# Values of three attention layers in plain fp32 on two 64-column tiles, with new call orders

## Chip, cores and metric

The kernel runs on one core of a Trainium2 chip. The metric is the device time of one launch in microseconds (us), as the median of several runs. The core has a matrix engine (TensorE, "PE" in the profile, its weight loads "PEld"), VectorE ("DVE"), ScalarE ("ACT"), GpSimd ("POOL") and SyncE ("SP").

## What is computed

One inference step of a backbone with four layers over 640 tokens (512 latent tokens, 128 context tokens) of 1024 features. Layers 0 and 3 have mixer A (sliding window, grouped queries, a sink logit per head), layer 1 mixer B (latent attention), layer 2 mixer C (normalised queries and keys, full attention over the latent tokens and the context). Each is followed by a squared-ReLU MLP; shift, scale and gate come from a conditioning vector (adaLN). All is fp32. The core of a mixer, cut to what matters here:

```
def attend(q, k, v, scale, sink=None, mask=None):
    s = jnp.einsum('bqhgd,bkhd->bhgqk', q, k) * scale
    if mask is not None:
        s = jnp.where(mask, s, NEG_INF)
    ...                       # softmax over keys, with the sink column
    return jnp.einsum('bhgqk,bkhd->bqhgd', p.astype(v.dtype), v)

for i in range(DEPTH):
    ...
    hp = modulate(rmsnorm(xp, norm_g[i, 0]), sh_p, sc_p)
    hs = modulate(rmsnorm(xs, norm_g[i, 0]), sh_s, sc_s)
    if kind == 0:
        op, k_ctx, v_ctx = mixer_a_context(hp, a_w_qkv[j], a_sink[j], a_w_o[j])
        os_ = mixer_a_latent(hs, cache_a_k[:, j], cache_a_v[:, j], a_w_qkv[j], a_sink[j], a_w_o[j], rows, cols)
    ...
    xs = xs + gt_s * os_
    xs = xs + gt2_s * sq_relu_mlp(modulate(rmsnorm(xs, norm_g[i, 1]), sh2_s, sc2_s), w_mlp_in[i], w_mlp_out[i])
```

There are 16 query heads of 64 features and 4 key/value heads; in mixer A a block of 128 queries sees at most three blocks of 128 latent keys and one of 128 context keys.

## The kernel before

**Split products.** Almost every matrix product is made of two-part numbers: an operand x is held as hi (a copy rounded to the type fp32r, one pass through TensorE) and lo = x - hi (also fp32r), and a product is three matmuls, hi·hi, hi·lo and lo·hi, into one accumulator. The hi part is made by a copy on ScalarE, the lo part by a subtraction on VectorE. Weights are loaded into `wraw`, split into pairs of tiles `wa`, and feed matmuls of 320 tokens (two halves of the 640).

**Attention of kinds A and C.** The sixteen heads are handled as eight pairs, class `Pair`. The steps of a pair: `qk` (scores), `mx`, `ex`, `rc`, `sc` (row maximum, exponential, reciprocal, scaling; GpSimd has a part of the scaling), then for each head e and group g of key blocks `tr` (transpose of the probabilities on TensorE into a PSUM bank of the pool `tb`), `hi` and `lo` (the split of the transposed tile from PSUM into two arena tiles), and `pv` (the product with the values, accumulated in the bank `V` over both heads of the pair). Kind A has four groups with together five key blocks of 512, 256, 256, 384 and 384 query columns per head; kind C has five groups of 512. The steps that begin with `z` do the same for the 128 context queries (`zt` transposes, `zh` and `zl` split, `zv` multiplies, `za` and `zb` put the result away, once for each head). `oh` and `ol` split the pair's output for the output projection. `fw`, `fh` and `fl` load and split weights of that projection meanwhile.

**Where the values lie.** In kind A the values of a key block are split into `VH` and `VL` with columns of zeros between the heads, so that a 128-column weight tile holds one head's 64 columns and 64 zeros, and both heads add into one bank of 128 partitions; a product is three matmuls. In kind C, `VS` holds the hi and lo columns of one head side by side (128 columns), so two matmuls do, and `pa` (ScalarE) and `pb` (VectorE) add the two halves afterwards; `ol` is on GpSimd there.

**What sets the order.** Calls to the engines are recorded by `Calls.keep` and made in another order by `replay`: for each phase ("0 qkv", "0 attn", "0 oproj" and so on) a table `ORDER` of written-out numbers gives the order, on all engines at once. In a phase of attention the calls are recorded in the order that `PLAN` gives: a list of steps, each with a lag in rounds behind the round's pair (`tr00.2` is worked for the pair two rounds back), and the table acts on that. Each engine then works through its own list in this order and waits where data isn't there. Since the calls are made in one place, all instructions in the trace have the line of `make`, L276, and are told apart by their tiles: `p` probabilities, `cst` the identity for transposes, `ar` arena tiles of 128 x 640, `ps` and `psl` PSUM banks, `x` the residual stream, `adaw` and `junk` adaLN weights and their reductions on VectorE.

Of the kernel before, what the change touches and what calls it, by code (L numbers as in the profile page):

```python
# [12 lines left out]
F32 = mybir.dt.float32  # L13
# [16 lines left out]
WCAP = 6  # L30
KIND = "ABCA"
# [10 lines left out]
ORDER = {  # L42
    "0 attn": """
# [19 lines left out]
    """,  # L63
    "0 oproj": """
# [9 lines left out]
    """,  # L74
    "0 qkv2": """
# [4 lines left out]
    """,  # L80
    "0 qkv": """
# [5 lines left out]
    """,  # L87
    "0 start": """
# [4 lines left out]
    """,  # L93
    "1 dq": """
# [108 lines left out]
    """,  # L203
}
ORDER = {n: [int(i) for i in o.split()] for n, o in ORDER.items()}

# [1554 lines left out]
```

## Time and profile before

| | us |
|---|---|
| median of 3 runs | 3064.46 (3064.37 to 3067.91) |
| profiled execution, own time | 3069.06 |
| its span | 3067.3 |
| TensorE busy | 2962.0 |
| VectorE busy | 2122.7 |
| ScalarE busy | 1339.0 |
| GpSimd busy | 548.0 |

The mean granted clock of TensorE over the profiled execution is 0.991 of full. The stages on the time axis: start and projections of layer 0 until about 154, its attention until 260, output projection and MLP until about 780; layer 1 until about 1590; layer 2's projections until 1699, its attention until about 1830, its MLP until about 2290; layer 3's projections until 2438, its attention until 2542, then its MLP and the end. A row of the timeline is a run of like instructions of one engine: start, duration from the first start to the last end, engine, line, operation, output<-inputs, rows*columns of the tile of TensorE, shape of the moving data, count, and in brackets the idle time ahead of it and what ended it. Records of matmuls overlap, since matmuls are pipelined: the distance between starts tells their price, not their durations. A plain fp32 matmul leaves two records, one of fp32r leaves one.

### The profile page before, as it was taken

How to read it: one execution, taken by the hardware profiler on the slowest of the kernel's cores; microseconds unless marked ns; L12 is line 12 of the kernel's file. 1: busy time of each engine (PE TensorE's matmuls, PEld its weight loads, DVE VectorE, ACT ScalarE, POOL GpSimd, SP SyncE). 2: the span in 40 equal slices, each digit the busy share in tenths (PEclk: the TensorE clock that was granted, in tenths of full speed). 3: DMA queues.
4: the chain of work that ended last, by engine and by line, in shares of the span. 5: the costliest groups of instructions: out<-in, count | busy, mean ns of one | idle time of the engine just before them, and what ended most of it. 6: DMA issues, size and time to landing. Idle time of an engine off the chain costs nothing. (4 is left out here: it accounts for less than half of the span.)

```text
span 3067.3 us, 52256 instructions
## 1 busy us (share of the span) xinstructions
PE 2962.0 (97%) x20250; PEld 2884.7 (94%) x20250; DVE 2122.7 (69%) x4605; ACT 1339.0 (44%) x2836; POOL 548.0 (18%) x713
## 2 busy tenths in 40 slices
PE   6999999999999999999998999999999999999998
PEld 4888999999999989999997889999999899999998
DVE  5696767666788887767469988776747896533434
ACT  3384522323487753322347883332233593322331
POOL 1162000000044341000003660000000370000000
PEclk9999999999999999999999999999999999999999
DMA  8303344442121134444211013444431102222221
GB/s 300 130 1 124 103 145 152 149 149 96 40 60 47 37 125 163 147 152 148 84 55 45 10 43 118 146 150 152 144 93 49 46 1 83 90 72 74 76 76 49
DMA packets 88602, 300.72 MB, mean 98 GB/s; under 512 B 10977, under 2 KB 15281, under 8 KB 87969
## 3 DMA queue, kind: packets, MB, share of 16 engines
q1 hardware_dynamic: 64112, 210.22, 20.6%
q0 software_dynamic: 24240, 87.16, 8.7%
q8 instruction: 159, 2.61, 0.3%
q14 instruction: 91, 0.74, 0.1%
HBM read 288.53 MB, written 3.56 MB: 95 GB/s over the span
## 5 line engine op out<-in xcount | busy, mean ns | idle before, releaser
L276 PE MATMUL ps<-ar,wa 128*128 128x320 f32 x6736 | 1139.2, 311 | 16.4 <-DVE wa L276 8.7
L276 PE MATMUL psl<-ar,wa 128*128 128x320 f32 x6408 | 1084.3, 310 | 1.9 <-DVE ar L276 1.6
L276 PEld LDWEIGHTS ps<-ar,wa 128*128 128x128 f32 x6736 | 1030.0, 189 | 20.9 <-DVE wa L276 9.5
L276 PEld LDWEIGHTS psl<-ar,wa 128*128 128x128 f32 x6408 | 979.4, 188 | 3.4 <-DVE ar L276 2.3
L276 ACT ACTIVATE wa<-wraw 128x1024 fp32r<-128x1024 f32 (+3 forms) x350 | 360.0, 1030 | 965.2 <-PE psl L276 440.2
L276 DVE TENSOR_TENSOR wa<-wraw,wa 128x1024 fp32r<-128x1024 f32 (+3 forms) x346 | 416.7, 1204 | 291.8 <-ACT wa L276 290.8
L276 DVE CUSTOM_DVE_ANT_0 junk<-adaw,cb 128x1024 bf16<-128x1024 f32 x304 | 373.4, 1228 | 9.4 <-DMA adaw<-ada 8.9
L276 PE MATMUL psl<-ex,wa 128*128 128x320 f32 x1320 | 322.9, 314 | 5.1 <-DVE wa L276 2.0
L276 PE MATMUL ps<-ex,wa 128*128 128x320 f32 x1304 | 318.1, 313 | 5.5 <-DVE wa L276 3.3
L276 POOL TENSOR_TENSOR p<-p,st 128x640 f32<-128x640 f32 (+2 forms) x256 | 277.0, 1104 | 180.0 <-DVE st L276 144.7
L276 POOL DMA_DIRECT2D adaw<-ada x152 | 80.5, 530 | 1051.4 <-DVE mod L276 983.9
L276 PE MATMUL psl<-wa,ar 128*128 128x320 f32 (+3 forms) x1024 | 236.2, 335 | 17.0 <-DVE st L276 7.5
L276 PEld LDWEIGHTS psl<-ex,wa 128*128 128x128 f32 x1320 | 229.1, 189 | 9.4 <-DVE wa L276 2.3
L276 DVE TENSOR_TENSOR ar<-ps,ar 128x512 fp32r<-128x512 f32 (+3 forms) x416 | 223.2, 560 | 19.8 <-ACT ar L276 16.3
L276 PEld LDWEIGHTS ps<-ex,wa 128*128 128x128 f32 x1304 | 225.5, 189 | 9.8 <-DVE wa L276 4.2
L276 ACT ACTIVATE ar<-ps 128x512 fp32r<-128x512 f32 (+5 forms) x452 | 208.5, 489 | 56.1 <-PE ps L276 50.7
L276 DVE SCALAR_TENSOR_TENSOR x<-ps,mod,x 128x320 f32<-128x320 f32 (+2 forms) x264 | 107.2, 436 | 180.8 <-PE ps L276 180.6
L276 DVE SCALAR_TENSOR_TENSOR x<-psl,mod,x 128x320 f32<-128x320 f32 (+2 forms) x240 | 98.7, 436 | 192.3 <-PE psl L276 192.2
L276 ACT ACTIVATE p<-p,st 128x640 f32<-128x640 f32 (+2 forms) x256 | 190.6, 748 | 18.7 <-DVE st L276 8.6
L276 PEld LDWEIGHTS psl<-wa,ar 128*128 128x128 f32 x1024 | 166.0, 193 | 30.7 <-DVE st L276 14.9
L276 PE MATMUL ps<-cst,p 128*128 128x128 f32 x1088 | 155.2, 274 | 5.6 <-DVE wa L276 2.6
L276 DVE TENSOR_TENSOR usq<-relu 128x320 f32<-128x320 f32 x256 | 124.5, 487 | 44.5 <-ACT relu L276 42.6
(205 smaller groups left out, 2817.6 us busy)
## 6 DMA issues: line engine op xcount, KB each, us to landing
adaw<-ada POOLq DMA_DIRECT2D x152, 512.0 KB, 4.3
wraw<-win SPq DMA_DIRECT2D x128, 512.0 KB, 3.3
wraw<-wout SPq DMA_DIRECT2D x128, 512.0 KB, 3.3
wraw<-qkv SPq DMA_DIRECT2D x36, 512.0 KB, 3.6
wa<-adan SPq DMA_DIRECT2D x24, 512.0 KB, 5.1
wraw<-wo SPq DMA_DIRECT2D x24, 512.0 KB, 3.7
adaw<-ada SPq DMA_DIRECT2D x16, 512.0 KB, 8.4
ar<-wa SPq DMA_DIRECT2D x64, 80.0 KB, 2.1
```

The source lines that it names most:

```text
L276: return m(*a, **k)
```

## The change

In the attentions of layers 0, 2 and 3 neither the values nor the transposed probabilities are split. The values lie in one fp32 tile `V` of 128 x 6 x 256, written by one copy on ScalarE per token block and by the transfer of the cached values directly. A transposed group is copied once, by step `cp`, from PSUM into an fp32 tile of a new pool `pt` (eight arena tiles turned to fp32 and `PT` = 5 or 6 new ones): odd groups on VectorE, even groups on ScalarE. `pv` is one step for the whole pair: plain fp32 matmuls whose weight tile is the 64 columns of one head, with the two heads of the pair alternating and writing to partitions 0 to 63 and 64 to 127 of the same bank. `zc`, `zv`, `za` and `zb` are made alike. `oh` and `ol` read the bank, `ol` on VectorE in both kinds. The zero columns, `VS` and the adding of halves are gone from kinds A and C; class `PairB` (layer 1) keeps the split steps.

```
+PT = {"A": 5, "C": 6}
...
+    def cp(self, e, g):
+        t = self.T[e, g]
+        ps = t[0]
+        t[0] = self.k.pt.popleft()
+        if g % 2:
+            self.nc.vector.tensor_copy(out=t[0][:, :t[1]], in_=ps[:, :t[1]])
+        else:
+            self.nc.scalar.activation(t[0][:, :t[1]], ps[:, :t[1]], AF.Copy)
+        self.k.tb.append(ps)
+
+    def pv(self):
+        k, nc = self.k, self.nc
+        self.V = k.vb.popleft()
+        last = {"A": 3, "C": 4}[k.kind]
+        for g in range(last + 1):
+            G = self.groups(g)
+            o = 0
+            for i, (kb, b0, b1) in enumerate(G):
+                n = (b1 - b0) * P
+                for e in (0, 1):
+                    nc.tensor.matmul(self.V[64 * e:64 * e + 64, b0 * P:b1 * P], self.v(kb, e), self.T[e, g][0][:, o:o + n], start=g + i == 0, stop=g == last and i == len(G) - 1)
+                o += n
+            k.pt += [self.T.pop((e, g))[0] for e in (0, 1)]
+
+    def v(self, kb, e):
+        c = (self.pr // 4 * 2 + e) * 64
+        return self.k.V[:, kb, c:c + 64]
...
+    def zc(self):
+        self.zt_ = self.k.pt.popleft()
+        self.nc.scalar.activation(self.zt_[:, :256], self.ZT[:, :256], AF.Copy)
+        self.k.tb.append(self.ZT)
+
+    def zv(self):
+        k = self.k
+        o = self.ZO = k.tb.popleft()
+        for e in (0, 1):
+            self.nc.tensor.matmul(o[64 * e:64 * e + 64, :P], self.v(5, e), self.zt_[:, e * P:e * P + P], start=True, stop=True)
+        k.pt.append(self.zt_)
...
                 def values():
-                    cv, sv = csv or (cks(), self.rps()[:, :256])
-                    nc.gpsimd.dma_start(cv, a["cv"][l])
+                    nc.gpsimd.dma_start(self.V[:, 2, :], a["cv"][l])
...
-                        if tb < 4:
-                            self.v_put(KB_OF_TB[tb], ps[:, :256])
-                        else:
-                            nc.scalar.activation(sv, ps[:, :256], AF.Copy)
-                            nc.gpsimd.dma_start(a["sv"][l], sv)
-                            self.v_put(5, sv)
+                        nc.scalar.activation(self.V[:, KB_OF_TB[tb], :], ps[:, :256], AF.Copy)
+                        if tb == 4:
+                            nc.gpsimd.dma_start(a["sv"][l], self.V[:, 5, :])
```

`PLAN` for kinds A and C is rewritten with the new steps; the largest lag falls from four rounds to three. The table of every phase of `ORDER` is new, except "2 oproj" and "3 oproj", which are the same, and layer 1's attention keeps its plan.

What moves, on TensorE in layer 0's attention, in the middle of a round, before (`VH` and `VL` the split values, `ar` the split probabilities, `cst,p` transposes, `psl` scores):

```order
L276 MATMUL ps_72<-cst,p_4_1466 128x128 x2
L276 MATMUL ps_74<-ar_95,VH_487 128x384
L276 MATMUL ps_74<-ar_94,VH_487 128x384
L276 MATMUL ps_74<-ar_94,VL_488 128x384
L276 MATMUL psl_1_79<-wa_111,ar_99 128x512
L276 MATMUL psl_1_79<-wa_113,ar_99 128x512
L276 MATMUL ps_74<-ar_83,VH_487 128x384
L276 MATMUL ps_74<-ar_82,VH_487 128x384
L276 MATMUL ps_74<-ar_82,VL_488 128x384
```

and after:

```order
L261 MATMUL ps_73<-cst,z_0_1474 128x128 x2
L261 MATMUL ps_74<-ar_1461,V_487 64x512
L261 MATMUL ps_74<-ar_1465,V_487 64x512
L261 MATMUL ps_74<-ar_1462,V_487 64x256
L261 MATMUL ps_74<-ar_1466,V_487 64x256
L261 MATMUL ps_74<-ar_1462,V_487 64x256
L261 MATMUL ps_74<-ar_1466,V_487 64x256
L261 MATMUL ps_74<-ar_1463,V_487 64x384
L261 MATMUL ps_74<-ar_1467,V_487 64x384
L261 MATMUL ps_74<-ar_1464,V_487 64x384
L261 MATMUL ps_74<-ar_1468,V_487 64x384
L261 MATMUL ps_72<-t_0_1469,V_487 64x128 x2
```

The products with the values, spread before between transposes and scores in threes, now stand in one block of ten and two more for the context.

On VectorE at the end of layer 0's attention and the start of its output projection, before (`junk` with `ISA` a reduction for adaLN, `wa<-wraw` the lo part of a projection weight):

```order
L276 TENSOR_TENSOR wa_117<-wraw_1_62,wa_116 128x1024
L276 TENSOR_TENSOR ar_83<-ps_72,ar_82 128x384
L276 TENSOR_TENSOR ar_85<-ps_73,ar_84 128x256
L276 TENSOR_TENSOR ar_109<-ps_71,ar_108 64x128
L276 TENSOR_TENSOR ar_87<-ps_74,ar_86 128x512
L276 TENSOR_TENSOR ar_87<-ps_72,ar_86 64x128 x2
L276 ISA junk,mod_0_169<-adaw_0_2674,cb 128x1024
```

and after:

```order
L261 TENSOR_TENSOR wa_117<-wraw_1_62,wa_116 128x1024
L261 COPY t_2_1471<-ps_73 128x384
L261 TENSOR_TENSOR wa_993<-wraw_0_61,wa_992 128x1024
L261 TENSOR_TENSOR ar_105<-ps_74,ar_104 128x512
L261 TENSOR_TENSOR ar_105<-ps_72,ar_104 128x128
L261 TENSOR_TENSOR wa_111<-wraw_0_61,wa_110 128x1024
L261 ISA junk,mod_0_169<-adaw_0_2428,cb 128x1024
```

Behind the last row eight reductions follow in both; before, two weight splits (the one shown and one three rows ahead of it) stand close ahead of them, after, three, the last of them next to the reductions.

On ScalarE in layer 3's projections, where the value weights are split, before (`wa<-wraw` the hi part of a weight, `ar<-rpq` and `rpq` the rotary chain of queries and keys):

```order
L276 ACTIVATE wa_1005<-wraw_0_61 128x1024
L276 ACTIVATE ar_85<-rpq_1_21711 64x320
L276 ACTIVATE ar_84<-rpq_1_21711 64x320
L276 ACTIVATE ar_96<-rpq_0_21710 64x320
L276 ACTIVATE ar_97<-rpq_0_21710 64x320
L276 ACTIVATE rpq_1_21711<-psl_3_17223 128x128
L276 ACTIVATE ar_97<-rpq_1_21711 64x320
L276 ACTIVATE ar_96<-rpq_1_21711 64x320
L276 ACTIVATE wa_110<-wraw_1_62 128x1024
```

and after:

```order
L261 ACTIVATE ar_106<-rpq_0_21242 64x320
L261 ACTIVATE ar_107<-rpq_0_21242 64x320
L261 ACTIVATE wa_994<-wraw_0_61 128x1024
L261 ACTIVATE rpq_1_21243<-psl_1_16750 128x128
L261 ACTIVATE wa_110<-wraw_1_62 128x1024
L261 ACTIVATE ar_107<-rpq_1_21243 64x320
L261 ACTIVATE ar_106<-rpq_1_21243 64x320
```

The two copies of the value weights stood with seven operations of the rotary chain between them; now there is one.

## Rows read from the trace of the kernel before

**Rows 1.** The page, busy us, share of the span and instructions of each engine.

```profile
PE 2962.0 (97%) x20250; PEld 2884.7 (94%) x20250; DVE 2122.7 (69%) x4605; ACT 1339.0 (44%) x2836; POOL 548.0 (18%) x713
```

**Rows 2.** Stretches: window, length, busy PE PEld DVE ACT POOL, granted clock, DMA.

```profile
170.00:250.00 80.00, 79.12 (x527) 71.36 (x526) 74.34 (x235) 72.88 (x208) 58.12 (x90) 1.00 0.01 1
1712.00:1820.00 108.00, 107.03 (x703) 94.69 (x702) 105.49 (x274) 105.84 (x250) 81.47 (x71) 1.00 0.02 6
```

**Rows 3.** Timeline of TensorE in layer 0's attention: start, us, instructions.

```profile
217.37 0.64 PE L276 MATMUL ps<-ar,VH 128*128 128x512 f32 x2
...
218.08 0.49 PE L276 MATMUL ps<-cst,p 128*128 128x128 f32 x3
...
225.87 0.40 PE L276 MATMUL ps<-ar,VH 128*128 128x256 f32 x2
...
226.22 0.60 PE L276 MATMUL ps<-cst,p 128*128 128x128 f32 x4
226.57 0.49 PE L276 MATMUL ps<-ar,VH 128*128 128x256 f32 x2
...
227.02 0.51 PE L276 MATMUL ps<-ar,VH 128*128 128x384 f32 x2
...
227.54 0.51 PE L276 MATMUL ps<-ar,VH 128*128 128x384 f32 x2
```

**Rows 4.** Timeline of TensorE and its weight loads at adaLN matmuls on column tiles.

```profile
29.85 0.64 PE L276 MATMUL ps<-adaw,cs 128*32 128x256 f32 x8 [3.10 <-DMA adaw<-ada]
...
54.34 1.34 PE L276 MATMUL psl<-ar,wa 128*128 128x320 f32 x8
55.60 1.07 PE L276 MATMUL ps<-wa,cs 128*32 128x256 f32 x16
56.60 0.41 PE L276 MATMUL ps<-ex,wa 128*128 128x320 f32 x1
56.85 0.31 PE L276 MATMUL ps<-ar,wa 128*128 128x320 f32 x1
...
55.60 0.59 PEld L276 LDWEIGHTS ps<-wa,cs 128*32 128x32 f32 x16 [0.19 <-issue]
56.60 0.19 PEld L276 LDWEIGHTS ps<-ex,wa 128*128 128x128 f32 x1 [0.41 <-ACT ar L276]
```

**Rows 5.** Groups by shape: out<-in, count | busy us, mean ns | idle before.

```profile
L276 DVE TENSOR_TENSOR ar<-ps,ar 128x512 fp32r<-128x512 f32 x224 | 148.7, 683 | 11.5 <-ACT ar L276 9.9
L276 ACT ACTIVATE ar<-ps 128x512 fp32r<-128x512 f32 x224 | 128.2, 594 | 30.9 <-PE ps L276 27.3 <-ACT ar L276 0.6 <-ACT p L276 0.5
```

**Rows 6.** Timeline of TensorE and VectorE at the start of layer 0's output projection.

```profile
281.09 13.11 PE L276 MATMUL ps<-ar,wa 128*128 128x320 f32 x70 [6.66 <-DVE wa L276]
...
278.67 1.22 DVE L276 CUSTOM_DVE_ANT_0 junk<-adaw,cb 128x1024 bf16<-128x1024 f32 x1
...
279.82 1.22 DVE L276 TENSOR_TENSOR wa<-wraw,wa 128x1024 fp32r<-128x1024 f32 x1
```

**Rows 7.** Timeline of TensorE at layer 3's values.

```profile
2422.20 1.44 PE L276 MATMUL psl<-wa,ar 128*128 128x256 f32 x3 [3.27 <-ACT wa L276]
2425.01 2.72 PE L276 MATMUL psl<-wa,ar 128*128 128x256 f32 x11 [1.38 <-DVE wa L276]
```

**Rows 8.** Timeline of TensorE at the first scores of layer 2's attention.

```profile
1699.30 1.92 PE L276 MATMUL psl<-wa,ar 128*128 128x320 f32 x8 [3.52 <-DVE VS L276]
```

**Rows 9.** Timeline of TensorE and VectorE at layer 0's last query columns.

```profile
144.21 0.90 PE L276 MATMUL ps<-ex,wa 128*128 128x320 f32 x2 [3.34 <-DVE wa L276]
...
142.94 1.22 DVE L276 TENSOR_TENSOR wa<-wraw,wa 128x1024 fp32r<-128x1024 f32 x1
```

**Rows 10.** Stretches with half clock: window, length, busy PE PEld DVE ACT POOL, clock, DMA.

```profile
144.00:150.00 6.00, 5.79 (x22) 5.80 (x23) 4.82 (x12) 2.15 (x5) 1.64 (x2) 0.50 0.29 87
1699.00:1707.00 8.00, 6.77 (x25) 5.85 (x26) 4.65 (x13) 3.73 (x9) 1.18 (x1) 0.57 0.00 1
2422.00:2430.00 8.00, 6.42 (x26) 5.70 (x27) 5.48 (x12) 3.10 (x8) 1.17 (x2) 0.50 0.29 84
```

More of the change, by code (lines that the diff above doesn't have):

```diff
@@ L42 @@
 ORDER = {
-    "0 attn": """
[19 rows of a table removed]
+    "1 dq": """
[6 rows of a table added]
+    """,
+    "3 attn": """
[15 rows of a table added]
+    """,
+    "2 attn": """
[15 rows of a table added]
+    """,
+    "0 attn": """
[15 rows of a table added]
+    """,
+    "1 oproj": """
[9 rows of a table added]
+    """,
+    "3 qkv": """
[9 rows of a table added]
+    """,
+    "2 qkv": """
[13 rows of a table added]
+    """,
+    "0 qkv": """
[5 rows of a table added]
     """,
     "0 oproj": """
[9 rows of a table removed]
[9 rows of a table added]
     """,
     "0 qkv2": """
[4 rows of a table removed]
-    """,
-    "0 qkv": """
[5 rows of a table removed]
[4 rows of a table added]
     """,
     "0 start": """
[4 rows of a table removed]
-    """,
-    "1 dq": """
[6 rows of a table removed]
-    """,
-    "1 oproj": """
[9 rows of a table removed]
-    """,
-    "2 attn": """
[21 rows of a table removed]
[4 rows of a table added]
     """,
@@ L146 @@
     """,
-    "2 qkv": """
[13 rows of a table removed]
-    """,
-    "3 attn": """
[19 rows of a table removed]
-    """,
     "3 oproj": """
@@ L192 @@
     """,
-    "3 qkv": """
[9 rows of a table removed]
-    """,
 }
@@ L463, in tr @@
             self.k.px.append(self.X.pop((e, j)))
-    def hi(self, e, g):
+    def cp(self, e, g):
         t = self.T[e, g]
-        t += self.k.alloc(2)
-        self.nc.scalar.activation(t[2][:, :t[1]], t[0][:, :t[1]], AF.Copy)
-    def lo(self, e, g):
-        ps, n, th, tl = self.T[e, g]
-        self.nc.vector.tensor_tensor(out=tl[:, :n], in0=ps[:, :n], in1=th[:, :n].bitcast(F32), op=ALU.subtract)
+        ps = t[0]
[4 more added lines that the diff above has]
+            self.nc.scalar.activation(t[0][:, :t[1]], ps[:, :t[1]], AF.Copy)
         self.k.tb.append(ps)
-    def pv(self, e, g):
+    def pv(self):
         k, nc = self.k, self.nc
-        _, _, th, tl = self.T.pop((e, g))
-        first = g == 0 and (k.stack or e == 0)
-        last = g == {"A": 3, "B": 5, "C": 4}[k.kind] and (k.stack or e == 1)
-        if first:
-            self.V = k.vb.popleft()
-        G = self.groups(g)
-        o = 0
-        for i, (kb, b0, b1) in enumerate(G):
-            n = (b1 - b0) * P
-            ms = k.v_parts(self.hs[e], kb, th, tl)
-            for j, (v, t) in enumerate(ms):
-                nc.tensor.matmul(self.V[:, b0 * P:b1 * P], v, t[:, o:o + n], start=first and i + j == 0, stop=last and j == len(ms) - 1 and i == len(G) - 1)
-            o += n
-        k.free([th, tl])
+        self.V = k.vb.popleft()
[12 more added lines that the diff above has]
+        return self.k.V[:, kb, c:c + 64]
     def out(self, i):
@@ L495, in out, with oh, ol @@
         return self.O[self.pr][i]
-    def pa(self, e):
-        if e == 0:
-            self.o32 = self.k.po.popleft()
-        r = 64 * e
-        self.nc.scalar.activation(self.o32[r:r + 64, :], self.V[64 - r:128 - r, :], AF.Copy)
-    def pb(self, e):
-        o = self.o32[64 * e:64 * e + 64, :]
-        self.nc.vector.tensor_tensor(out=o, in0=self.V[64 * e:64 * e + 64, :], in1=o, op=ALU.add)
-        self.k.vb.append(self.V)
-    def oh(self):
-        self.nc.scalar.activation(self.out(0)[:, :TS], self.o32 if self.k.stack else self.V, AF.Copy)
-    def ol(self):
-        k = self.k
-        e, src, free = (self.nc.gpsimd, self.o32, k.po) if k.stack else (self.nc.vector, self.V, k.vb)
-        e.tensor_tensor(out=self.out(1)[:, :TS], in0=src, in1=self.out(0)[:, :TS].bitcast(F32), op=ALU.subtract)
-        free.append(src)
+    def oh(self):
+        self.nc.scalar.activation(self.out(0)[:, :TS], self.V, AF.Copy)
+    def ol(self):
+        self.nc.vector.tensor_tensor(out=self.out(1)[:, :TS], in0=self.V, in1=self.out(0)[:, :TS].bitcast(F32), op=ALU.subtract)
+        self.k.vb.append(self.V)
     def fw(self, u):
@@ L564, in zt, with za @@
         self.k.pz.append(self.Z)
+    def zc(self):
[8 more added lines that the diff above has]
+        k.pt.append(self.zt_)
+    def za(self):
+        self.nc.scalar.activation(self.out(0)[:, TS:], self.ZO[:, :P], AF.Copy)
@@ new lines, in zb, with __init__, has, hi @@
+    def zb(self):
+        self.nc.vector.tensor_tensor(out=self.out(1)[:, TS:], in0=self.ZO[:, :P], in1=self.out(0)[:, TS:].bitcast(F32), op=ALU.subtract)
+        self.k.tb.append(self.ZO)
+class PairB(Pair):
+    def __init__(self, k, pr, Q, O):
+        super().__init__(k, pr, Q, O)
+        self.g = k.pairs_[-1].g if pr % 2 else {}
+        self.w, self.K, self.Y = None, {}, {}
+        if pr == 0:
+            self.g["w"], self.w = [[None, None, *k.ws.get()] for _ in range(2)]
+            k.ws.out -= 2
+    def has(self, n):
+        if n in ("gw", "gh", "gl", "wd", "wh", "wl") and self.pr == 0:
+            return False
+        return {"g": self.pr % 2 == 0, "v": self.pr % 2 == 0, "y": self.pr == 4, "f": self.pr == 7, "x": self.pr == 7}.get(n[0], True)
+    def hi(self, e, g):
+        t = self.T[e, g]
+        t += self.k.alloc(2)
+        self.nc.scalar.activation(t[2][:, :t[1]], t[0][:, :t[1]], AF.Copy)
+    def lo(self, e, g):
+        ps, n, th, tl = self.T[e, g]
+        self.nc.vector.tensor_tensor(out=tl[:, :n], in0=ps[:, :n], in1=th[:, :n].bitcast(F32), op=ALU.subtract)
+        self.k.tb.append(ps)
+    def pv(self, e, g):
+        k, nc = self.k, self.nc
+        _, _, th, tl = self.T.pop((e, g))
+        first, last = g == 0, g == 5
+        if first:
+            self.V = k.vb.popleft()
+        G = self.groups(g)
+        o = 0
+        for i, (kb, b0, b1) in enumerate(G):
+            n = (b1 - b0) * P
+            ms = k.v_parts(self.hs[e], kb, th, tl)
+            for j, (v, t) in enumerate(ms):
+                nc.tensor.matmul(self.V[:, b0 * P:b1 * P], v, t[:, o:o + n], start=first and i + j == 0, stop=last and j == len(ms) - 1 and i == len(G) - 1)
+            o += n
+        k.free([th, tl])
+    def pa(self, e):
+        if e == 0:
+            self.o32 = self.k.po.popleft()
+        r = 64 * e
+        self.nc.scalar.activation(self.o32[r:r + 64, :], self.V[64 - r:128 - r, :], AF.Copy)
+    def pb(self, e):
+        o = self.o32[64 * e:64 * e + 64, :]
+        self.nc.vector.tensor_tensor(out=o, in0=self.V[64 * e:64 * e + 64, :], in1=o, op=ALU.add)
+        self.k.vb.append(self.V)
+    def oh(self):
+        self.nc.scalar.activation(self.out(0)[:, :TS], self.o32, AF.Copy)
+    def ol(self):
+        k = self.k
+        self.nc.gpsimd.tensor_tensor(out=self.out(1)[:, :TS], in0=self.o32, in1=self.out(0)[:, :TS].bitcast(F32), op=ALU.subtract)
+        k.po.append(self.o32)
@@ L577, in zv @@
         th, tl = self.zt_
-        c = k.vp0 + (self.pr % 2 if k.kind == "B" else self.pr // 4) * P
+        c = self.pr % 2 * P
         o = self.ZO = k.tb.popleft()
@@ L592, in zb @@
             self.k.tb.append(self.ZO)
-class PairB(Pair):
-    def __init__(self, k, pr, Q, O):
-        super().__init__(k, pr, Q, O)
-        self.g = k.pairs_[-1].g if pr % 2 else {}
-        self.w, self.K, self.Y = None, {}, {}
-        if pr == 0:
-            self.g["w"], self.w = [[None, None, *k.ws.get()] for _ in range(2)]
-            k.ws.out -= 2
-    def has(self, n):
-        if n in ("gw", "gh", "gl", "wd", "wh", "wl") and self.pr == 0:
-            return False
-        return {"g": self.pr % 2 == 0, "v": self.pr % 2 == 0, "y": self.pr == 4, "f": self.pr == 7, "x": self.pr == 7}.get(n[0], True)
     def gw(self):
@@ L1029, in v_parts @@
     def v_parts(self, h, kb, th, tl):
[L1035 to L1049 removed]
+        c = kb * 512 + h % 4 // 2 * 256 + h % 2 * P
+        v = self.VS[:, c:c + P]
+        return (v, tl), (v, th)
+    def v_tiles(self, pool, l):
+        if self.kind == "B":
+            self.VH, self.VL = [pool.tile([P, 256], F32R, name=f"V{n}{l}") for n in "HL"]
             self.VS = pool.tile([P, 2560], F32R, name=f"VS{l}")
         else:
[L1052 to L1058 removed]
+            self.V = pool.tile([P, 6, 256], F32, name=f"V{l}")
     def v_place(self, kb, src):
         if kb == 5:
[L1063 removed]
+            return [self.VH, self.VL], src
         src = src.rearrange("p (k t d) -> p k t d", t=2, d=64)
[L1065 to L1068 removed]
+        v = self.VS[:, kb * 512:kb * 512 + 512].rearrange("p (k t d) -> p k t d", t=4, d=64)
+        return [v[:, :, 0::3, :], v[:, :, 1:3, :]], src
     def attend(self, Q, O):
@@ L1121, in mixer_ac @@
                 cks = self.ring(tp, "ck", 2 * P, 2 if l else 1)
-                csv = [tp.tile([P, 256], F32, name=n, bufs=1) for n in ("cv", "sv")] if l else None
                 Q = [None] * 16
@@ L1238, in mixer_ac @@
                 self.sts = Ring([self.sp.tile([P, 3, 10], F32, name=f"st{l}_{i}") for i in range(4)])
-                self.po = deque(self.sp.tile([P, TS], F32, name=f"o{l}_{i}") for i in range(3 if self.stack else 0))
+                pt = self.renew(self.alloc(8), F32)
+                self.pt = deque(pt + [self.sp.tile([P, TS], F32, name=f"t{l}_{i}") for i in range(PT[kind])])
                 self.pz = deque(self.sp.tile([P, 2, 129], F32, name=f"z{l}_{i}") for i in range(2))
@@ L1249, in mixer_ac @@
                 self.psum(False)
+                self.free(self.renew(pt, F32R))
                 self.wfree(self.KH + self.KL)
```

42 lines of the change are left out of this document (8 added, 34 removed), and 222 rows, old and new, of the table ORDER.

## The prediction

> **What bounds the kernel now.** I read the busy times of the engines first: TensorE is busy for 2962.0 us of the 3067.3 us span [rows 1], so the time is the sum of what TensorE must stream plus its idle time and its slow-clock stretches. The attention of layer 0 is next, as a table of stretches: in 80.00 us of it TensorE is busy 79.12, VectorE 74.34, ScalarE 72.88, GpSimd 58.12; in 108.00 us of layer 2's attention the four have 107.03, 105.49, 105.84 and 81.47, both at full clock [rows 2]. So TensorE ends these stages too, but two other engines are within 7 to 9% of it in layers 0 and 3, and within 2% in layer 2. Last I read the timeline at the places where the new call orders differ from the old and TensorE stands still or runs at half clock: [rows 6 to 9], with the clock in [rows 10].
>
> **TensorE's price of a values block, before.** The starts of consecutive blocks give it [rows 3]: a block of three matmuls over 512 columns takes 218.08 - 217.37 = 0.71 us, over 256 columns 226.22 - 225.87 = 0.35, over 384 columns 227.54 - 227.02 = 0.52. That is 0.455 ns per column and pass. In layers 0 and 3 a head has one block of 512, two of 256, two of 384: 0.71 + 0.70 + 1.04 = 2.45 us; a pair 4.90, and its context block (three of 256) 0.35, so 5.25. Sixteen pairs: 84.0 us. In layer 2 a pair has 20 matmuls of 512 columns (stacked values need two passes per key block and head) at 0.71 / 3 = 0.237, so 4.73, plus 0.35: 5.08, and eight pairs 40.7 us. Together 124.7 us.
>
> **The same, after.** No row has 64-column tiles in plain fp32, but the adaLN matmuls are plain fp32 on 32-column tiles, four at once, each with its own moving data [rows 4]. Eight records (four matmuls of 256 columns, two records each) take 0.64 us, sixteen take 1.07: 0.43 us for four more matmuls, or 1.68 ns per column for all four together. They run side by side: one after the other each would have 0.42 ns per column, less than a one-pass matmul needs. I take 1.68 ns per column for two tiles together. Layers 0 and 3: 1792 columns x 1.68 = 3.01 us, context 128 x 1.68 = 0.215, so 3.23 per pair, 51.6 for sixteen. Layer 2: 2560 x 1.68 = 4.30, plus 0.215: 4.52, 36.1 for eight. The saving is (84.0 - 51.6) + (40.7 - 36.1) = **37.0 us**. The bounds of it: tiles that don't run together (the slower rival), and a gain of nothing more, since the streaming itself can't be shorter than the rows' rate.
>
> **Going in and out of tiles.** At the one tiled block between full-array matmuls [rows 4], eight 320-column matmuls ahead of it take 1.26 us where 8 x 320 x 0.455 ns = 1.16: 0.10 more. The tiled stretch takes 1.00 until the next full matmul where two waves stream 0.86: 0.14 more; the first matmul behind takes 0.25 instead of 0.146: 0.10 more. So 0.34 per block, 24 blocks: **+8.2**. The Trainium skill ("TensorEngine Tiling (Array Packing)", Key Properties) says that a change of tiling mode drains TensorE; the trace agrees, with 0.34 as its price here.
>
> **Switches between transposes and products.** The first 256-column block behind transposes takes 227.02 - 226.57 = 0.45 instead of 0.35 [rows 3]: 0.10 per switch. In TensorE's order, the attentions of layers 0, 2 and 3 have 163 such switches before and 109 after, since a pair's products stand in one block: 54 x 0.10 = **-5.4**. TensorE's own content thus changes by -37.0 + 8.2 - 5.4 = **-34.2 us**.
>
> **The other engines in attention.** The split of a 512-column tile costs ScalarE 594 ns and VectorE 683 ns [rows 5]; after, one of the two engines makes one copy. VectorE's eight subtractions of a pair (in layers 0 and 3 about 5.2 us: the 683 ns scaled to 512, 384 and 256 + 256 columns) become four copies, at most 2.6 us if a copy costs what a subtraction does. Of a pair's time of 106 / 8 = 13.3 us VectorE had 0.93, so 12.3; it gets 9.7 of a new pair time near 11.3, so 0.86. ScalarE loses four of eight copies in the same way. In layer 2 both lose this and the two operations that add the halves, while VectorE takes one subtraction (about 0.68) from GpSimd. None becomes the bound, but the chain from a score to its product is longer than the block it feeds only by the plan's lag, which falls from four rounds to three. I allow **+4** for it, between 0 and 17 (half of the saving).
>
> **The rewritten orders, where TensorE stands still before.** (a) Layer 0's output projection: TensorE idles 6.66 us behind VectorE's weight split, which starts at 279.82 behind eight adaLN reductions of 1.22; the 70 matmuls behind it take 13.11 where 70 x 0.146 = 10.2 [rows 6], so 9.6 us are lost. After, a third weight split stands ahead of the eight reductions on VectorE; one weight tile feeds 48 matmuls (eight slices, three passes, two halves), 7.0 us at 0.146, a little more than the idle time. What is late next is the split behind the reductions. I take -8. (b) Layer 3's values: idle 3.27 and 1.38, behind ScalarE's weight copy and then VectorE's subtraction [rows 7], then 8 us at clock 0.50 with 6.42 busy, of which half is lost [rows 10]: 7.9. After, the two weight copies are one operation apart on ScalarE instead of seven. I take -6. (c) Entry of layer 2's attention: idle 3.52 behind VectorE's value splits [rows 8], then 8 us at 0.57 with 6.77 busy, 2.9 lost: 6.4. After there are no value splits on VectorE. I take -5. (d) Layer 0's last query columns: idle 3.34 behind a weight split at 142.94 that stands behind the rotary chain [rows 9], then 6 us at 0.50 with 5.79 busy, 2.9 lost: 6.2. After, the weight split stands earlier. I take -4.5. Sum **-23.5** of 30.1, bounded by 0 and -30.1. Where orders of the same length are dealt anew, new waits of this size can come at other places; I set **+8** against it, one place like (a) or (b), with 0 and 24 (three) as bounds.
>
> **Sum.** -34.2 + 4 - 23.5 + 8 = -45.7. Against the profiled execution's 3069.06 us: 3023.4. That execution was 4.6 us above the median 3064.46, so the median goes to 3018.8, **3019**.
>
> **Rivals.**
> *Orders give nothing* (new waits of the same size elsewhere): -34.2 + 4 = -30.2, 3034 us, or 3041 with one place more. For it: a wait with its half clock costs 6 to 10 us at each of four places, and every table is new. Against: each named wait has a named cover. Chance 0.13.
> *Attention becomes bound by its chain*: half of the 34.2 is lost, -28.6, 3036 us. For it: layer 2 has VectorE and ScalarE within 2% of TensorE [rows 2]. Against: both lose more work than TensorE. Chance 0.13.
> *Weight loads stand open.* A tiled block reads 12 weight tiles per pair. In the tiled stretch of [rows 4] sixteen loads of 32 columns take 0.59 and the tiles' streaming isn't stretched, so they lie under it. If each of 288 loads stood open, at 0.074 (twice 0.59 / 16) to 0.19 (a full load in the same rows), this would add 21 to 54, middle 38: 3057. The rows speak against it. The Trainium skill ("TensorE: Matmul & The Clock Gate", Part 3, The mechanism) says that a weight load overlaps running matmuls only where the row groups differ, and here they don't; the row shows the loads overlapped with equal row groups, so I give this rule a chance of 0.05.
> *Slower: the two tiles of a pair run one after the other.* Then each column costs 2 x 1.68 ns, +3.23 x 16 + 4.52 x 8 = +88 on the sum: 3107 us. It decides against the change as soon as less than about half of a wave overlaps (45.7 / 88). For it: two heads write the same bank and the same columns of it, at other partitions, which no row shows for 64. Against: the four tiles of [rows 4] do overlap fully. Chance 0.05.
> *Better than 3004*: waits gone entirely and no new ones, chance 0.04.
>
> **How the numbers follow.** Forecast (3004 to 3032) 0.60, orders 0.13, chain 0.13, open loads 0.05, tiles in turn 0.05, better 0.04. The range for 8 in 10 takes the forecast, most of both middle rivals and part of the better case: 2998 to 3042. A measurement of this kernel can tell 0.2%, 6.1 us, from no change. Faster: forecast, orders, chain, better, and half of the open loads, 0.92; within 0.2%: 0.03; slower: the tiles in turn, 0.05.
>
> **What the profile after would show.** Right: a pair's values block of layers 0 and 3 about 3.2 us with the records of both tiles starting together, 4.5 in layer 2; layer 0's attention about 15 us shorter; no idle time of TensorE ahead of layer 0's output projection; full clock in the three stretches of [rows 10] and behind (a). Wrong: blocks of twice that length (tiles in turn); gaps between the waves (loads); idle time of TensorE on copies, or behind VectorE and ScalarE, between blocks (chain); new waits of 3 us and more in qkv and projections (orders).

## The result, and the profile after

The changed kernel takes 3020.03 us (3018.78 to 3020.94, 4 runs) where the kernel before takes 3066.07: a ratio of 0.9849, 95% interval 0.9832 to 0.9867, so 46 us less. The forecast was 3019. The kernels below were each run beside the kernel before, which took 3066.9 to 3067.4 us there, and 3063.4 beside old_2qkv. The profiled execution took 3020.94 us, 48.1 less than the one of before.

The page's busy times, the row that answers to [rows 1]:

```profile
PE 2940.3 (97%) x20114; PEld 2813.5 (93%) x20114; DVE 2031.8 (67%) x4419; ACT 1276.0 (42%) x2694; POOL 534.3 (18%) x701
```

TensorE is still the bound, with 21.7 us less busy time; the other 27 us of the gain are idle time. The attentions of layers 0, 2 and 3 as three stretches, first of the kernel before, then after, cut at TensorE's first score and last values product (window, length, busy time of PE PEld DVE ACT POOL, granted clock, DMA):

```profile
153.80:260.20 106.40, 102.15 (x669) 90.76 (x667) 98.04 (x303) 91.56 (x259) 68.22 (x113) 1.00 0.03 7
1695.78:1830.07 134.29, 127.40 (x810) 111.64 (x810) 127.74 (x326) 122.75 (x288) 93.88 (x79) 0.97 0.03 9
2440.24:2541.13 100.89, 99.71 (x664) 90.90 (x662) 94.95 (x293) 90.39 (x258) 66.82 (x105) 1.00 0.02 6
```

```profile
152.80:243.38 90.58, 88.09 (x593) 64.13 (x593) 75.57 (x253) 75.35 (x220) 67.00 (x112) 1.00 0.02 6
1673.93:1798.55 124.62, 122.74 (x820) 90.92 (x818) 87.36 (x252) 94.25 (x234) 82.75 (x72) 1.00 0.02 8
2405.03:2494.39 89.36, 88.14 (x594) 63.52 (x593) 73.29 (x249) 74.69 (x218) 66.58 (x107) 1.00 0.02 5
```

They are 15.8, 9.7 and 11.5 us shorter, and 1.0 of idle time behind the third is gone: 38.0 of the 48.4 by which the span fell. TensorE's busy time falls by 14.1, 4.7 and 11.6, and VectorE and ScalarE, at 0.86 to 0.95 of the stretch before, are at 0.70 to 0.84.

A values block of layer 0 on TensorE's timeline answers to [rows 3]: all of a pair's products, with the context, lie between 201.80 and 205.18.

```profile
201.49 0.38 PE L261 MATMUL ps<-cst,z 128*128 128x128 f32 x2
201.80 1.08 PE L261 MATMUL ps<-ar,V 128*64 128x512 f32 x4
202.71 1.03 PE L261 MATMUL ps<-t,V 128*64 128x256 f32 x8
203.57 1.68 PE L261 MATMUL ps<-ar,V 128*64 128x384 f32 x12
205.18 1.09 PE L261 MATMUL ps<-cst,p 128*128 128x128 f32 x8
```

The tile form reads 128*64. 3.38 us for a block of 1792 + 128 columns: 3.23 at 1.68 ns per column, and 0.15 of what going in and out costs.

Behind the attention of layer 0 TensorE has no idle time where [rows 6] has 6.66 us, and the clock stays full (stretch of the projection):

```profile
262.00:290.00 28.00, 28.00 (x193) 28.00 (x193) 22.25 (x39) 10.15 (x17) 0.69 (x2) 1.00 0.50 164
```

There is also a new wait. At the norm ahead of layer 2's projections TensorE waits 1.64 us and then runs at half clock for about 10 us; the first row is its timeline, the second the stretch:

```profile
1568.49 1.16 PE L261 MATMUL ps<-dg,cst 128*128 128x128 f32 x4 [1.64 <-DVE dg L261]
...
1560.00:1580.00 20.00, 17.08 (x83) 14.98 (x83) 13.53 (x42) 10.60 (x29) 0.00 (x0) 0.74 0.19 55
```

Laid side by side by TensorE's landmarks, the two traces differ so (us, after less before): up to the first attention -1.0; attention 0 -15.8; output projection 0 up to its norm -8.2; from there to layer 1's attention -4.2; from there to layer 2's attention **+7.3**; attention 2 -9.7; to layer 3's attention -3.7; attention 3 with the wait behind it -12.5; the rest -0.7. The +7.3 is the balance of 833 us: 1.5 in layer 1's attention, 3.0 from there to the norm ahead of layer 2's projections, 2.8 from that norm to layer 2's first score.

### The profile page after: what moved, and what is told of

Read it like the earlier page. It is cut to its first block, busy times and chain, and to the rows that moved or that the text cites. A ratio compares the mean times of both kernels' runs of the same rounds, so it can differ in the third digit from the quotient of the medians.

```text
span 3018.9 us, 51500 instructions
## 1 busy us (share of the span) xinstructions
PE 2940.3 (97%) x20114; PEld 2813.5 (93%) x20114; DVE 2031.8 (67%) x4419; ACT 1276.0 (42%) x2694; POOL 534.3 (18%) x701
## 5 line engine op out<-in xcount | busy, mean ns | idle before, releaser
L261 PEld LDWEIGHTS ps<-ar,wa 128*128 128x128 f32 x6736 | 1029.5, 188 | 10.6 <-DVE wa L261 2.6
L261 ACT ACTIVATE wa<-wraw 128x1024 fp32r<-128x1024 f32 (+2 forms) x350 | 359.8, 1030 | 956.8 <-PE psl L261 442.8
L261 DVE TENSOR_TENSOR wa<-wraw,wa 128x1024 fp32r<-128x1024 f32 (+2 forms) x346 | 412.9, 1194 | 294.8 <-ACT wa L261 294.0
L261 ACT ACTIVATE ar<-ps 128x512 fp32r<-128x512 f32 (+7 forms) x282 | 130.3, 479 | 71.3 <-PE ps L261 67.6
L261 PEld LDWEIGHTS ps<-cst,p 128*128 128x128 f32 x1088 | 125.7, 140 | 18.2 <-DVE wa L261 3.9
```

Of the source, the lines that this page charges most:

```text
L261: return m(*a, **k)
```

## Experiments

**Code and orders apart.** My theory: the 38 us inside the attentions are the new code's, the net 10.5 outside are the orders'. Rival: the new code brought both, since it leaves VectorE and ScalarE less behind. In the first kernel all tables outside the attentions are the new ones, renumbered for the old calls; in the second the reverse. In the first, the order no longer fits the storage that the calls were dealt, so it doesn't compute the layers' values, but every instruction is made.

```
 order_only: kernel before
-    "0 start", "0 qkv", "0 qkv2", "0 oproj", "1 dq", "1 oproj", "2 qkv", "3 qkv": before's orders
+    the same eight: after's orders
 code_only: kernel after
-    the same eight: after's orders
+    the same eight: before's orders
```

> The kernel before with the new call orders of all eight phases outside the attentions (the value subtractions, which the new orders don't have, stand right behind their copies); the attentions and their code are the old ones. My theory: between the attentions the changed kernel won 10.5 us net (1.0 before the first attention, 12.4 from its end to layer 1's attention, 3.7 between the attentions of layers 2 and 3, 0.7 at the end, less 7.3 lost from layer 1's attention to layer 2's), and the orders alone did this: 3066 - 10.5 = 3055, between 3050 and 3061. Rival: the new code did it, since it leaves VectorE and ScalarE free and values without subtractions: 3066 plus or minus 3.

Measured: 3056.74 us against 3067.38 of before beside it, ratio 0.9965 (0.9952 to 0.9978): -10.6 where -10.5 was expected.

> The changed kernel with the old call orders of the same eight phases (calls that are gone left out); new code and new plan in the attentions. My theory (orders outside, TensorE content and the missing value splits inside): 3020 + 10.5 = 3030.5, between 3025 and 3036. Rival (the new code did it all): 3020 plus or minus 3.

Measured: 3028.93 (3025.9 to 3031.4), 8.9 over the changed kernel, ratio to before 0.9873 (0.9857 to 0.989); by the ratios, which set each beside its own kernel before, 7.4. So the parts add up: about 38 us for code and plan inside the attentions (no run takes these two apart), 7 to 11 for the orders outside. The rival falls in both.

**One of the four places.**

```
 kernel after
-    "0 oproj": after's order
+    "0 oproj": before's order
```

> The changed kernel with only the order of layer 0's output projection put back. My theory: TensorE waits again for the weight split behind the eight adaLN reductions and then runs at half clock, 6.7 + 2.9 us: 3020 + 8 to 10 = 3028 to 3030. Rival: VectorE comes out of the new attention with less behind it, so that the wait is gone in either order: 3020 to 3022.

Measured: 3028.22 (3027.8 to 3030.4), +8.2. TensorE's timeline has the wait of [rows 6] again, 5.84 instead of 6.66, and VectorE's weight split again stands at the end of the reductions:

```profile
263.30 12.14 PE L253 MATMUL ps<-ar,wa 128*128 128x320 f32 x70 [5.84 <-DVE wa L253]
...
260.87 1.22 DVE L253 CUSTOM_DVE_ANT_0 junk<-adaw,cb 128x1024 bf16<-128x1024 f32 x1
262.02 1.22 DVE L253 TENSOR_TENSOR wa<-wraw,wa 128x1024 fp32r<-128x1024 f32 x1
...
260.00:270.00 10.00, 6.70 (x35) 6.71 (x36) 5.08 (x8) 1.34 (x2) 0.92 (x2) 0.66 0.61 217
```

The last row is the stretch around its end, at clock 0.66. The new attention doesn't remove this wait; the new order of the output projection does, in which a third weight split stands ahead of the reductions.

**Is the +7.3 the orders', too?** Of the eight tables, the two of the phases that lost time are put back.

```
 mix: kernel after
-    "1 oproj", "2 qkv": after's orders
+    "1 oproj", "2 qkv": before's orders
```

> The changed kernel with the old orders of layer 1's output projection and layer 2's projections, the two phases in which it lost time (1.8 and 2.8 us, with new half-clock stretches of 3.4 us at 1104.67 and 10.24 us at 1579.12 in its trace, and 1.2 between). My theory: the losses belong to these orders: 3020 - 4 to - 6 = 3014 to 3016. Rival: half-clock stretches come where they come, with either order: 3020 plus or minus 2, with the stretches at other places; or the old waits for weight splits in layer 2 (1.25 and 2.01 us) come back and eat the gain.

(The times 1104.67 and 1579.12 there are on the clock record's own axis; on the profile's they are 10.5 us less.) Measured: 3013.74 (3012.4 to 3016.1), 6.3 under the changed kernel, ratio to before 0.9826 (0.9811 to 0.984). At the same norm TensorE waits 0.45 us and keeps its clock:

```profile
1559.98 0.88 PE L241 MATMUL ps<-dg,cst 128*128 128x128 f32 x6 [0.45 <-DVE dg L241]
...
1552.50:1572.50 20.00, 19.55 (x131) 18.73 (x131) 17.38 (x51) 12.88 (x30) 0.00 (x0) 1.00 0.25 83
```

So this kernel beats both, though the intervals of its ratio and of the changed kernel's overlap a little; mix_start below, which holds the same two tables, comes out at the same time. Three kernels divide and extend it:

```
 old_2qkv: kernel after
-    "2 qkv": after's order
+    "2 qkv": before's order
 mix_start: mix
-    "0 start": after's order
+    "0 start": before's order
 mix_hyb: mix
-    "2 qkv": before's order
+    "2 qkv": before's order to the end of the norm, after's behind it
```

> The changed kernel with the old order of layer 2's projections alone; layer 1's output projection keeps the new one (mix has both old). In the traces mix won 5.3 us from the norm behind layer 1's attention to the next norm, lost 1.8 to 2.1 in the projections of layer 2 behind it, and layer 1's output projection took 46 us in both. My theory: the whole gain of mix is the norm at the head of layer 2's phase, where TensorE waits 0.45 instead of 1.64 us and keeps its full clock: as mix, 3012 to 3015. Rival: layer 1's output projection has half of it: 3016 to 3018.

> The kernel of mix with the old order of the start as well. In the trace of the kernel with all old orders the second norm of the start stood 1.9 us earlier than in the changed kernel's. My theory: 3013.7 - 1.9 = 3011.8. Rival: what the start gains is lost in the projections behind it (the first transposes of the attention stood 0.6 us later there, seen from that norm), or hidden in half-clock stretches at the start: 3013 to 3017.

> The kernel of mix with layer 2's projections ordered as before only up to the end of the norm, and in the changed kernel's order behind it. In the traces mix won 3.5 us at that norm and lost 1.8 us in the projections behind it. My theory: both parts keep their own time: 3013.7 - 1.8 = 3011.9. Rival: the old waits and half-clock stretches come with the join: 3013 to 3017.

Measured: 3016.51 (3014.3 to 3020.7), 3013.51 (3011.4 to 3018.3) and 3014.03 (3013.1 to 3018.1). The first lies where the rival put it. By its ratio, 0.9847 (0.9831 to 0.9862), it is no faster than the changed kernel, since the kernel before took 3063.4 beside it.

The traces show why the norm isn't the whole gain. From the first sum of squares of that norm to the first transposes of layer 2's attention, the changed kernel first, then mix (rows of TensorE, then the stretch):

```profile
1541.63 0.83 PE L261 MATMUL ps<-ones,acc 128*128 128x1 f32 x6
1683.89 0.84 PE L261 MATMUL ps<-cst,p 128*128 128x128 f32 x4
...
1541.63:1683.89 142.26, 128.66 (x793) 117.90 (x793) 122.74 (x288) 90.75 (x212) 44.55 (x47) 0.95 0.12 40
```

```profile
1536.62 0.83 PE L241 MATMUL ps<-ones,acc 128*128 128x1 f32 x6
1615.85 0.41 PE L241 MATMUL psl<-ex,wa 128*128 128x320 f32 x1 [1.25 <-ACT wa L241]
1618.42 0.56 PE L241 MATMUL psl<-ex,wa 128*128 128x320 f32 x2 [2.01 <-DVE wa L241]
1640.29 1.44 PE L241 MATMUL ps<-hsq,cst 128*128 128x320 f32 x2 [2.37 <-ACT hsq L241]
1677.37 0.60 PE L241 MATMUL ps<-cst,p 128*128 128x128 f32 x4
...
1536.62:1677.37 140.75, 127.34 (x794) 117.47 (x794) 123.83 (x288) 92.05 (x212) 43.76 (x49) 0.96 0.12 41
```

The old table wins 1.5 us here and no more (old_2qkv: 140.7): the wait at the norm goes, but old waits for split weights and for the norms of queries and keys come back, with half-clock stretches of their own. The 3.5 us that the expectations saw won ahead of the norm's second sum and the 1.8 lost behind it are largely one shift: TensorE is busy throughout between the two sums, 24.5 us with 170 matmul records in the changed kernel and 21.0 with 145 in mix. From the last transposes of layer 1's attention to the first sum the changed kernel takes 483.2 us, old_2qkv 483.0, mix 481.2 and mix_start 480.2, so the old table of layer 1's output projection wins 2 to 3. The rival of old_2qkv thus holds, and two tables account for 3 to 5 us; the rest by which mix's profiled execution is ahead lies where both kernels have the same tables.

mix_start and mix_hyb gain nothing. The start up to the first transposes takes 158.2 to 163.0 us in the traces of all kernels here, with either order, so 1.9 us there aren't told from scatter. mix_hyb takes 140.5 between the two landmarks above, where its theory needs 139: the 1.8 us that it was to win were part of the shift.

**Do the two tiles run side by side?** Three kernels price the block. The first deals the products of a pair anew:

```
-                for e in (0, 1):
-                    nc.tensor.matmul(self.V[64 * e:64 * e + 64, b0 * P:b1 * P], self.v(kb, e), ...
+        for e in (0, 1):
+            for g in range(last + 1):
+                ...
+                    nc.tensor.matmul(self.V[64 * e:64 * e + 64, b0 * P:b1 * P], self.v(kb, e), ...
```

> The changed kernel with the ten (layer 2: ten) products of a pair dealt anew: all five of head 0 first, then all five of head 1, so that neighbours in the order use the same 64 columns. Same matmuls, same tiles, same result. My theory: two tiles run side by side only as neighbours in the order, so each column of a pair costs 2 x 1.68 ns: + 3.01 x 16 + 4.30 x 8 = 82.6, 3103 us (3095 to 3108). Rival: TensorE runs a tile's matmul beside an earlier one of the other tile wherever it stands in its queue: 3020 to 3030.

Measured: 3065.8 (3063.6 to 3071.1), +45.8: the whole gain of the change gone by an order of ten matmuls, but little more than half of what my theory gives. TensorE's timeline of a block whose head 0 reads `t` tiles and head 1 `ar` tiles shows why:

```profile
182.54 2.26 PE L261 MATMUL ps<-t,V 128*64 128x512 f32 x7
184.32 0.64 PE L261 MATMUL ps<-ar,V 128*64 128x512 f32 x1
184.64 0.49 PE L261 MATMUL ps<-t,V 128*64 128x384 f32 x1
184.80 0.59 PE L261 MATMUL ps<-ar,V 128*64 128x512 f32 x1
184.96 0.49 PE L261 MATMUL ps<-t,V 128*64 128x384 f32 x1
185.23 0.38 PE L261 MATMUL ps<-ar,V 128*64 128x256 f32 x1
185.28 0.49 PE L261 MATMUL ps<-t,V 128*64 128x384 f32 x1
185.44 2.32 PE L261 MATMUL ps<-ar,V 128*64 128x256 f32 x11
187.69 1.09 PE L261 MATMUL ps<-cst,p 128*128 128x128 f32 x8
```

The seven records of the first row are three whole matmuls of head 0 and the first record of its fourth. Head 1's first starts beside that fourth at 184.32, while head 0's fifth has yet to run (184.96). The next block has the same distance, 1.78 us (194.44 to 196.22). So in these blocks a matmul starts while one matmul of the other tile ahead of it still waits its turn, not while two do. The block takes 5.15 us (182.54 to 187.69) instead of 3.38; + 1.77 x 16 = 28.3 in layers 0 and 3, the rest in layer 2, whose stretch from first to last transpose grows from 109.6 to 127.9. Both theories were off: overlap needs near neighbours in the order, though not the nearest.

The second has no column tiles at all, the third has every product twice:

```
 full_width
-  self.V[64 * e:64 * e + 64, b0 * P:b1 * P], self.v(kb, e)
+  self.V[:, b0 * P:b1 * P], self.k.V[:, kb, self.pr // 4 * P:self.pr // 4 * P + P]
 ...                      # the context products alike
 twice
-                for e in (0, 1):
+                for r, e in ((0, 0), (0, 1), (1, 0), (1, 1)):
 ...                      # start and stop to match
```

> The changed kernel with weight tiles of all 128 columns (both heads' values at once) for each product, context products too, so that nothing runs in column tiles; both heads' results are added into one bank, so the output isn't the attention's. My theory: the same 82.6 us plus 8 x 3 x 0.215 = 5.2 for the context, less what going in and out of tiles costs. Of that I took 0.34 at 24 blocks = 8.2; layer 2 has its context block apart, so 32 blocks, 10.9. So 3020 + 87.8 - 10.9 = 3097 (3090 to 3103), below by_head. Rival: in and out of tiles costs nothing here, and the transposes and scores around the blocks are dearer for another reason: 3107 to 3110, above by_head.

> The changed kernel with every product of a pair's values block made twice (the sum is doubled, the context products are not), as alternating tiles. My theory: TensorE still ends the attention and a block costs 3.01 and 4.30 us, so doubling it adds all of it: + 82.6, 3103 us (3097 to 3108). Rival: VectorE, ScalarE or the chain from score to copy has become the bound, so that part of the added work lies under waits: less than 3070.

Measured: 3094.06 (3093.6 to 3095.5), +74.0, and 3101.41 (3095.7 to 3105.2), +81.4 where 82.6 was expected. The blocks on TensorE's timeline, full_width first (207.78 to 214.25: 6.47 us), then twice (210.03 to 216.43: 6.40):

```profile
207.78 1.88 PE L261 MATMUL ps<-ar,V 128*128 128x512 f32 x4
209.50 1.89 PE L261 MATMUL ps<-t,V 128*128 128x256 f32 x8
211.23 3.19 PE L261 MATMUL ps<-ar,V 128*128 128x384 f32 x12
214.25 1.04 PE L261 MATMUL ps<-cst,p 128*128 128x128 f32 x8
```

```profile
210.03 1.94 PE L261 MATMUL ps<-ar,V 128*64 128x512 f32 x8
211.80 1.90 PE L261 MATMUL ps<-t,V 128*64 128x256 f32 x16
213.53 2.97 PE L261 MATMUL ps<-ar,V 128*64 128x384 f32 x20
216.43 1.09 PE L261 MATMUL ps<-cst,p 128*128 128x128 f32 x8
```

6.45 us is what 2 x (1792 + 128) columns at 1.68 ns take, so a plain fp32 matmul costs the same with 128 columns of weights as with 64, and two tiles cost what one does. The added work of twice is paid almost in full (81.4 of 82.6): TensorE still ends these stages. full_width gives a price of going in and out by subtraction: 87.8 of streaming was added by that rate, 74.0 paid; if nothing else differs, the 13.8 are 32 stretches at 0.43 us where I had 0.34. It is also 27 us slower than the kernel before (ratio 1.0089, 1.0074 to 1.0104): unsplit products without the tiles lose.

**Fewer ways in and out.** In layer 2 the context product has a stretch of tiles to itself. In the next kernel it stands at the next pair's block. It doesn't compute the layers' latent values, since the moved steps no longer fit the storage that they were dealt; every instruction is made.

```
 mix_zv: mix, PLAN "C" and its order
-        ... tr04.1 cp04.1 zv.2 za.2 zb.2 oh.2 ol.2 ... mx11.0 pv.1 qk13.0
+        ... tr04.1 cp04.1 oh.2 ol.2 ... mx11.0 zv.2 pv.1 za.2 zb.2 qk13.0
```

> The kernel of mix with one move in layer 2's attention: the context product of a pair (two matmuls on 64-column tiles, in mix alone between scores and transposes) stands right in front of the next pair's values block, so that seven of sixteen stretches of column tiles are gone. My theory: each way in and out of tiles costs TensorE 0.34 us, or 0.43 as full_width gave over 32 stretches: 7 x 0.34 to 7 x 0.43 = 2.4 to 3.0 less than mix's 3013.7, so 3010.7 to 3011.3. Rival: the way in and out lies under waits that are there anyway (for copies and banks): 3013 to 3014.5.

Measured: 3017.08 (3012.8 to 3018.3), not faster than mix, and by the median above the rival's range too. Layer 2's attention from the first score to the last values product, mix first, as stretches:

```profile
1665.90:1791.83 125.93, 123.66 (x820) 92.34 (x818) 88.13 (x252) 94.42 (x235) 82.78 (x72) 0.99 0.02 7
```

```profile
1666.95:1795.55 128.60, 123.08 (x819) 91.94 (x817) 87.59 (x252) 95.13 (x235) 82.79 (x72) 0.99 0.02 6
PE ps L224 <- DVE st L224: 1.4, 1, 1.4
PE ps L224 <- POOL p L224: 1.1, 2, 0.9
```

TensorE's busy time falls by 0.6 us, not by the 2.4 to 3.0 of the price, and its idle time grows from 2.3 to 5.5, in part behind softmax statistics and scaled probabilities, which the two rows of waits show (total, times, longest). So this kernel doesn't confirm the price. That the chain through the softmax stands close behind TensorE in layer 2 is what the waits suggest.

**How much slack have the other engines?**

```
 copies_act
-        if g % 2:
-            self.nc.vector.tensor_copy(out=t[0][:, :t[1]], in_=ps[:, :t[1]])
-        else:
-            self.nc.scalar.activation(t[0][:, :t[1]], ps[:, :t[1]], AF.Copy)
+        self.nc.scalar.activation(t[0][:, :t[1]], ps[:, :t[1]], AF.Copy)
```

> The changed kernel with all copies of transposed probabilities on ScalarE, none on VectorE. ScalarE is busy 75.35 of layer 0's 90.58 us of attention; four copies more per pair (two of 512 columns at 0.595, two of 384 at 0.480) make 2.15 x 8 = 17.2 more, 92.6, over TensorE's time. My theory (ScalarE and VectorE have about a sixth of slack in the changed kernel, and none of it is wasted when it's exceeded): ScalarE becomes the bound in layers 0 and 3, 2 to 6 us each, and layer 2 stays as it is (94.25 + 19 of 124.6): 3024 to 3032. Rival: the plan's lag of three rounds already leaves chains late, so that every added copy shows: more than 3040.

Measured: 3040.17 (3036.0 to 3047.3), +20.1, at the rival's edge. From the first to the last transpose, the attentions of layers 0, 2 and 3 take 84.7, 117.7 and 84.5 us instead of 77.4, 109.6 and 77.2. In the profiled execution (3047.27 us, the slowest of four) TensorE waits longest in total for copies on ScalarE (first row), and ScalarE isn't even full in layer 0 (second):

```profile
PE ps L261 <- ACT ar L261: 10.0, 17, 1.6
...
165.00:235.00 70.00, 65.38 (x431) 46.96 (x429) 41.77 (x161) 64.57 (x191) 50.70 (x87) 0.98 0.00 1
```

Layer 2, where I expected nothing, loses 8.1 at a ScalarE share of 0.86 (100.86 of 117.69 us). The share of busy time overstates the slack: a copy that queues behind exponentials is late though the engine has time to spare. The halves on two engines are part of what makes the change work.

## Why the prediction was right, point by point

**The price of a values block** held: 3.38 us with its way in where 3.23 plus a part of 0.34 was forecast, and the rate of 1.68 ns, read from 32-column tiles, is that of 64-column tiles too. by_head shows that it hangs on the order of heads, which I hadn't named as a condition. In layer 2 a block takes 4.45 (1724.91 to 1729.36) and the context, apart, 0.37 where 4.52 plus a part of 0.34 was forecast for both.

**The switches and ways in and out** were mis-sized, on TensorE's own work. TensorE's work in the three attentions fell by 30.3 us, of which 2.9 is the half clock of [rows 10] at layer 2's entry, so 27.4 where -34.2 was forecast. I counted 24 stretches of tiles; layer 2 has two per pair, so 32; at full_width's 0.43 they would cost 13.8 and not 8.2, which would be 5.6 of the 6.8 missing. The eight stretches that I left out are certain; the 0.43 is a subtraction, and mix_zv didn't bear it out, so the rest of the miss isn't settled.

**Waits inside the attentions** went the other way. I allowed +4 for a chain that might come late (in layer 2's plan the largest lag falls to two rounds, not three), and -5 for layer 2's entry. The idle time of the three stretches, with what lay behind the third, fell by 7.7 us, 5.0 of it in layer 2 [rows 8]. With the half clock the attentions gave -38.0 where the sum had -35.2: two errors, +6.8 in the work and -9.6 in waits and clock, that nearly cancel. VectorE's eight subtractions of a pair, put at 5.2 us, are four of 683 and four of 550 ns, 4.9 in all; nothing hangs on that.

**The four places.** (a) -8.2 measured, -8 forecast, and old_oproj0 gives +8.2 when it alone is undone. (b) -3.7, not -6: TensorE still waits 0.54, 1.11 and 0.52 us there, and some 7 of 10 us at half clock remain, against the forecast sign of full clock there. (c) As forecast: from the first score to the first transposes it is 5.2 us shorter (15.2 before, 10.0 after), with waits of 1.09 us and less. (d) -1.0, not -4.5: the wait of [rows 9] is gone, but waits of 1.87 at 127.47 and 1.74 at 152.80 stand in its stead; one trace can't size it, since the start scatters by 5 us. The rows of TensorE at (b) and (d) in the changed kernel, then a stretch of old_2qkv at (b):

```profile
2387.25 0.38 PE L261 MATMUL psl<-wa,ex 128*128 128x256 f32 x1 [1.11 <-DVE wa L261]
...
152.80 1.91 PE L261 MATMUL psl<-wa,ar 128*128 128x384 f32 x8 [1.74 <-ACT rpq L261]
...
2382.27 0.39 PE L249 MATMUL psl<-wa,ex 128*128 128x256 f32 x1 [1.11 <-DVE wa L249]
2370.00:2400.00 30.00, 27.02 (x201) 26.14 (x200) 26.36 (x61) 13.60 (x32) 8.55 (x13) 1.00 0.18 58
```

old_2qkv has the same tables and the same wait there, and its clock stays full; it takes 617.1 us from the last transposes of layer 2's attention to the first of layer 3's, the changed kernel 619.1. So half clock behind such a wait isn't fixed by the order.

**The allowance of +8** for new waits was met in size by +7.3 from layer 1's attention to layer 2's, but not as one place like (a) or (b): no new wait reaches 2 us, and the 7.3 are spread over 833 us. mix gets 3 to 5 of it back. Further 4.2 us came from layer 0's norm to layer 1's attention, which I hadn't looked at. Outside the attentions all orders together gave -10.5, and -8 - 6 - 4.5 + 8 is -10.5 too; order_only and code_only confirm the sum (-10.6, +8.9), but its parts agree only at (a). The mechanism held: less work for TensorE in the values products, and waits taken away by the orders apart from it. That the total came within 1 us is luck.

**The rivals.** Tiles in turn: blocks of twice the length cost +81.4 in twice; the blocks of 3.38 us rule it out for the order as written. Open weight loads: no gaps between the waves. The rule of the Trainium skill ("TensorE: Matmul & The Clock Gate", Part 3, The mechanism), by which loads overlap only where row groups differ, isn't what this trace shows: the block takes what its streaming takes, with 24 loads in it. Chain: no bound as it stands, but copies_act and mix_zv show it a few us behind.

## What to carry to other kernels

When two heads of 64 columns share TensorE, unsplit fp32 on two column tiles costs 1.68 ns per column for both, against 2 x 1.37 for three passes of split numbers each; it pays only if the two tiles' matmuls alternate in the order. Price the change of order apart from the change of code: put the old tables on the new code and the new tables on the old code, and compare stretches between two landmarks with the same work between them: the wait of 1.64 us at a norm, with 10 us at half clock behind it, looked like the whole loss, but undoing its table won 1.5 us, because old waits came back. An engine that is busy 0.8 to 0.9 of a stage has less slack than that says when its work stands in a chain.

## What I had not expected of the hardware

In by_head's blocks a matmul on one column tile started beside one of the other tile while one more matmul of that tile stood waiting ahead of it, and not earlier: head 1 began at 184.32, beside the fourth of head 0's five. A plain fp32 matmul takes as long with 64 columns of weights as with 128 (24 records one after the other in 6.47 us in full_width, 24 on two tiles in 3.38). Half-clock stretches (0.50) followed waits of less than 2 us, but not each time: behind the 1.64 us at 1568.49 TensorE ran some 10 us at 0.50, while in mix, with 0.45, the clock stayed at 1.00; behind the same wait of 1.11 us at (b) the changed kernel had half clock and old_2qkv didn't.
